# More warming matmuls, a later rotary sum, fuller early filler and spread residual transposes in a two-layer hybrid encoder

## The chip, the cores and the metric

The kernel runs on one core of one Trainium2 chip, as one program launched once. A core has five engines with an instruction stream each: TensorE (PE, matrix products and transposes), VectorE (DVE), ScalarE (ACT), GpSimd (POOL) and SyncE (SP, which here only issues DMAs). Streams run side by side and meet at semaphores. Data lie in on-chip memory, products accumulate in the eight banks of PSUM, and weights come from the chip's main memory by DMA. The metric is the device time of one execution in microseconds (us); the median of the runs counts. The profile is one execution; PE's granted clock is part of it (1.00 is full, 0.50 half).

## The reference

Input: x of 512 tokens by 1024 features in float32, with the parameters of two layers. The tokens form a grid of 8 rows by 64 columns. Cut to what matters:

```
h = x
# layer 0
hn = rmsnorm(h, norm_mix[0])
qa, ka, va, cq, ckv, kr = split(hn @ w_in)                 # 1024 x 1440
qa = axial_rope(rmsnorm(qa per head)); ka = the same       # 8 heads, 2 kv heads of 64
oa = softmax(qa ka^T / 8) va                               # all 512 tokens
qb = rmsnorm(cq) @ w_uq;  kvb = rmsnorm(ckv) @ w_ukv       # 8 heads, 64 + 32 rotary
ob = softmax([q_nope, rope(q_rope)] [k_nope, rope(kr)]^T / sqrt(96)) vb
h = h + concat(oa, ob) @ w_out
h = h + relu(rmsnorm(h) @ w_up)^2 @ w_down                 # width 4096
# layer 1
q, k, v = split(rmsnorm(h, norm_mix[1]) @ w_qkv)           # 16 heads of 64
per query: a window of 8 rows x 16 columns of keys (clamped), softmax(q k^T / 8 + bias) v
h = h + o @ w_out
h = h + relu(rmsnorm(h) @ w_up)^2 @ w_down
return rmsnorm(h, final_norm)
```

The rotary scheme multiplies a vector by a cosine and its partner (the other half of a group of 32) by a sine, and adds the two.

## The kernel before

**Products.** A float32 product is made from two-part operands: each operand is split into a high part (rounded to fp32r) and the rest, and three matmuls stand for one product: high by high, high by low, low by high (`mm3`, L422 to L425 for the projections, L1366 to L1368 for the last down product, L311 to L313 in the other MLP parts). A matmul of 128x128 against 512 columns is the usual piece. Weights come in chunks: SP issues the DMA into `raw` (L180), ACT copies the high part `whi` (L189), DVE or POOL subtracts to get the low part `wlo` (L190, L200). There are four raw buffers and three of each part (`chunk`, L173).

**Order.** The order on each engine isn't that of the text. A scheduler takes the program's operations and lays out each engine's stream by its own model of when each is ready, so that an edit may or may not move an instruction. PSUM's banks are shared out by role: three `mm` banks for products, two `s` banks for scores, two `t` banks for transposes, one `o` bank for outputs and odds and ends. `Fill` keeps generators of products and lays them between attention steps, as many as a credit in us allows; a product of three matmuls counts 0.69.

**Beginning.** `idle_work` (L133) issues matmuls of ones by ones before any data is there. The gains `norm_mix` are turned by one transpose (L142) and copied to `gT` (L143). `make_x(k)` (L457 to L467) turns a block of x by four transposes (L461), and ACT (L465) and DVE (L466) split it, times the gain; DVE keeps the raw turn as `hT` (L467). `load_w(k)` (L619) brings one 128x768 chunk of `w_in`. Then `first_product` (L990) runs the first projection with six banks, eight steps along the depth each; `norm()` (L1012) is called inside of it, which sums squares over partitions by products with a column of ones (L443) and so gets the row factors. Layer 1's first projection goes through `norm()` as well.

**Layer 0, heads A.** `heads_A` (L903) runs eight heads in four units of two. At the first head of a unit it starts the next unit's rotary: `rope_q(t + 1)` (L524). `rope` (L473 to L486) issues eight DMAs on SP that bring the partners (L479), the product with the cosine, the product with the sine (L484, on POOL when `far`), and the sum on DVE (L485). The result is split by ACT and DVE (L537) and three SP DMAs put the parts where the two heads of the unit want them. `attend` (L832) makes a head in four score steps: scores (L876), the row's maximum in a DVE instruction that also copies them (L880), exponential on ACT, reciprocal (L883), scale on POOL (L884), then the turn of the weights by PE (L843), its split by ACT (L845) and DVE (L846), and the products with the values (L856 to L866). After each step it calls `done(i)`.

**Layer 1, heads C.** `projC(t)` makes q, k and v of two heads; k of each head is split (L1167, L1168) and copied to the other half of the partitions by a DMA on POOL's queue (L1170); v is turned by transposes (L1176). `attend_C` (L1187) runs 16 heads. Per head: scores of two blocks (L1201), the second half of the previous head's turns (`second`), filler (`step(n, 0)`), the previous head's value products (`finish`, L1235), scores of the other two blocks, filler, the first turns (L1220) and their split (L1224, L1225), filler. In front of every second head it makes sure that the filler of that pair's projection is done. `step` (L1295) sets the credit of a filler: 2.85 us, 5.6 from head 14 on, where the output projection is the filler.

**Last MLP.** `last_mlp` (L1316) makes the down product with the weights as the stationary operand: per step k along the depth four matmul triples j = 0..3. In the first group of steps, four transposes at a time (L1380) turn a block of the residual `hT` back into rows, into a `t` or an `mm` bank in turn, and ACT copies each block out (L1381). There are four blocks for each of two halves c.

Of the kernel before, what the change touches and what calls it, by code (L numbers as in the profile page):

```python
# [16 lines left out]
S = 512  # L17
# [18 lines left out]
def encoder_kernel(ctx: ExitStack, tc: tile.TileContext, ins, out, dbg=None):  # L36
# [51 lines left out]
    def ob():  # L88
        return bank("o", 1)
# [42 lines left out]

    def idle_work(n):  # L133
        b = ob()
        for _ in range(n):
            PE.matmul(b[:, 0:P], ones, ones, start=True, stop=True)

    idle_work(6)
    act0 = tiny(1)
    ACT.activation(act0, zeros, AF.Copy)  # L140
    gp = stb()
    PE.transpose(gp[:, 0:16], gs.t[0:16, 0:P], ident[0:16, 0:16])  # L142
    DVE.tensor_copy(gT[:, 0:16], gp[:, 0:16])  # L143

# [27 lines left out]

    def chunk(parts, nk, ncol, heads=None, eng=None):  # L173

# [13 lines left out]
        if heads is None:  # L188
            ACT.activation(hi[:, 0:m], raw[:, 0:m], AF.Copy)  # L189
            (eng or DVE).tensor_tensor(lo_[:, 0:m], raw[:, 0:m], f32(hi[:, 0:m]), op=ALU.subtract)  # L190
# [282 lines left out]
    def rope(src, cos, sin, mask, n=P, far=False):  # L473
# [9 lines left out]
        POOL.tensor_tensor(c[0:n, :], src[0:n, :], cos[0:n, :], op=ALU.mult)  # L483
        (POOL if far else DVE).tensor_tensor(sh[0:n, :], sh[0:n, :], sin[0:n, :], op=ALU.mult)  # L484
        DVE.tensor_tensor(c[0:n, :], c[0:n, :], sh[0:n, :], op=ALU.add)  # L485
        return c  # L486
# [37 lines left out]
    def rope_q(t):  # L524

        QA.append(Slot())
        rt = rope(QS[t // 2].t[:, S * (t % 2) : S * (t % 2) + S], cosA, sinA, sw16, far=t > 0)
        q = QA[t].pair()
        if t == 0:
            for e in range(2):  # L530
                a, z = 64 * e, 64 * (1 - e)
                ACT.activation(q[a : a + 64, e, :], rt[a : a + 64, :], AF.Copy)
                DVE.tensor_tensor(q[z : z + 64, e, :], rt[a : a + 64, :], f32(q[a : a + 64, e, :]), op=ALU.subtract)
        else:
            lo = scratch(F32R)
            ACT.activation(q[:, 0, :], rt, AF.Copy)
            DVE.tensor_tensor(lo, rt, f32(q[:, 0, :]), op=ALU.subtract)  # L537
            SP.dma_start(f32(q[0:64, 1, :]), f32(q[64:128, 0, :]))
            SP.dma_start(f32(q[64:128, 1, :]), f32(lo[64:128, :]))
            SP.dma_start(f32(q[64:128, 0, :]), f32(lo[0:64, :]))  # L540

# [77 lines left out]
    def load_w(k):  # L619
        W[k] = chunk([(0, 768, rows(w_in, k, 1)[:, :, 0:768])], 1, 768)  # L620

# [8 lines left out]
    load_x(1)  # L630
    make_x(0)
    make_x(1)
    load_w(2)
# [269 lines left out]
    def heads_A():  # L903
        for h in range(8):
            t, e, kv = h // 2, h % 2, h // 4
            if e == 0 and t < 3:
                rope_q(t + 1)
                if t == 2:
                    for s_ in QS + [rpA]:
                        s_.free()  # L910
            q, k = QA[t].pair(), KA[kv].pair()

            def done(i, t=t, e=e):
                if i == 3 and e:
                    QA[t].free()
                    if t % 2:
                        KA[t // 2].free()
# [72 lines left out]
    def first_product(l):  # L990
# [38 lines left out]
        def plain():  # L1029
            four = product(w, 0, xp, tiles(0, 512), ev, lambda n: [mmb(), mmb(), mmb(), sbk()])  # L1030
            two = product(w, 0, xp, tiles(512, 256), ev, lambda n: [sbk(), ob()], kstep=4)
            for n, _ in enumerate(four):
                if n == 11:
                    norm()
                if n == 14:
                    x7.sums(0, fill_x)
                    x7.sums(1, fill_x)
# [257 lines left out]
    def step(n, z):  # L1295
        if n == 14 and z == 0:
            for s_ in X:
# [3 lines left out]
            for cols in ([0, 1, 2], [3, 4, 5], [6, 7]):  # L1301
                out_proj(w_out1, 0, ok, cols, "out")
        fill.run(2.85 if n < 14 else 5.6)

# [11 lines left out]
    def last_mlp(l):  # L1316
# [37 lines left out]
        def down(k0, c, up, tail):  # L1354
# [5 lines left out]
            def run():  # L1360
# [9 lines left out]
                for k in range(nk - tail):  # L1370
                    for j in range(4):
                        use(k, j)
                        if k0 == 0:
                            later(c, 4 * k + j)
                        if k0 == 0 and k < 2 and j % 2:

                            i = 2 * k + j // 2
                            b = stb() if flip[0] == 0 else mmb()
# [89 lines left out]
```

## Time and profile before

| what | us |
|---|---|
| median of 3 runs | 1223.73 |
| the runs | 1222.79, 1223.73, 1228.44 |
| the profiled execution, whole time | 1228.26 |
| its span, first to last instruction | 1226.5 |
| mean granted clock of PE in it | 0.992 |
| PE busy | 1193.7 (97%) |
| DVE busy | 814.6 (66%) |
| ACT busy | 628.3 (51%) |
| POOL busy | 420.2 (34%) |

In the lines of the profile, each group is: engine, operation, output <- input by the names of the program, shape, and how often; L12 is line 12 of the kernel. In the timeline, the first number is the start in us from the start of the span, the second the length (of the whole run, where xN stands behind it), and a bracket holds how long the engine had stood idle just before and what ended it. In a list of waits, the three numbers are us in total, times, and the longest. A table of windows has, for each stretch, its length, then busy us and instructions of each engine, PE's clock as granted, the DMA share and GB/s. Matmuls overlap in the records: the pace is read from start to start.

The stages in this execution, by time: the first products up to about 45 us, layer 0's attention and output projection up to about 267, its MLP up to about 575, layer 1's first projection up to 637, its attention up to 851, and the output projection, the last MLP and the final norm up to 1226.5.

### The profile page before, as it was taken

How to read it: one execution, taken by the hardware profiler on the slowest of the kernel's cores; microseconds unless marked ns; L12 is line 12 of the kernel's file. 1: busy time of each engine (PE TensorE's matmuls, PEld its weight loads, DVE VectorE, ACT ScalarE, POOL GpSimd, SP SyncE). 2: the span in 40 equal slices, each digit the busy share in tenths (PEclk: the TensorE clock that was granted, in tenths of full speed). 3: DMA queues.
4: the chain of work that ended last, by engine and by line, in shares of the span. 5: the costliest groups of instructions: out<-in, count | busy, mean ns of one | idle time of the engine just before them, and what ended most of it. 6: DMA issues, size and time to landing. Idle time of an engine off the chain costs nothing.

```text
span 1226.5 us, 18425 instructions
## 1 busy us (share of the span) xinstructions
PE 1193.7 (97%) x6626; PEld 1004.5 (82%) x6626; DVE 814.6 (66%) x1433; ACT 628.3 (51%) x1051; POOL 420.2 (34%) x535
## 2 busy tenths in 40 slices
PE   9998999999999999999999999999989999999997
PEld 7676788887899889898877788777768988988985
DVE  4587888878677347457576677766974762763764
ACT  4477676664355226336345565554463641461543
POOL 3256242205374155254002222220333912723700
PEclk9999999999999999999999999999999999999999
DMA  6223314212235224247233334323222342241432
GB/s 235 71 57 102 74 48 129 69 52 69 77 88 154 86 61 139 85 139 241 85 88 106 108 108 117 108 95 103 70 68 60 96 155 61 80 157 48 121 121 69
DMA packets 107259, 122.69 MB, mean 100 GB/s; under 512 B 8115, under 2 KB 81120, under 8 KB 107168
## 3 DMA queue, kind: packets, MB, share of 16 engines
q1 hardware_dynamic: 104880, 116.15, 31.5%
q0 software_dynamic: 1536, 4.21, 1.4%
q10 hardware_dynamic: 752, 1.15, 0.3%
q8 instruction: 52, 0.85, 0.3%
q14 instruction: 39, 0.32, 0.1%
HBM read 104.32 MB, written 6.29 MB: 90 GB/s over the span
## 4 chain that ended last, share of the span: by engine, by line
PE 77%; DVE 8%; ACT 4%; POOL 3%; issue 3%; DMA 2%; SPq 1%; ACTq 0%; DVEq 0%; POOLq 0%
PE mm L425 8%; PE mm L423 8%; PE mm L424 8%; PE o L856 2%; PE s L876 2%; PE s L425 2%; PE s L424 2%; PE s L423 2%; PE t L843 2%; PE mm L1367 2%; PE mm L1368 2%; PE mm L1366 2%; PE mm L313 1%; PE mm L311 1%; PE mm L312 1%
## 5 line engine op out<-in xcount | busy, mean ns | idle before, releaser
L190 DVE TENSOR_TENSOR wlo<-raw,whi 128x1024 fp32r<-128x1024 f32 (+2 forms) x141 | 157.9, 1122 | 159.8 <-ACT whi L189 158.3
L189 ACT ACTIVATE whi<-raw 128x1024 fp32r<-128x1024 f32 (+2 forms) x145 | 137.2, 948 | 175.9 <-PE o L424 38.4
L423 PE MATMUL mm<-a,whi 128*128 128x512 f32 x524 | 213.3, 409 | 0.8 <-ACT whi L189 0.4
L424 PE MATMUL mm<-a,whi 128*128 128x512 f32 x524 | 209.2, 399 | 0.0
L425 PE MATMUL mm<-a,wlo 128*128 128x512 f32 x524 | 208.5, 400 | 0.1
L237 DVE TENSOR_TENSOR wlo<-raw,whi 128x896 fp32r<-128x896 f32 x104 | 130.7, 1257 | 106.2 <-ACT whi L236 105.8
L236 ACT ACTIVATE whi<-raw 128x896 fp32r<-128x896 f32 x104 | 98.8, 950 | 160.1 <-POOL raw L233 27.9
L231 POOL TENSOR_TENSOR raw<-raw 128x128 f32<-128x128 f32 x104 | 61.7, 593 | 267.5 <-DMA raw<-in_ffn_w_up_dram 221.1
L425 PEld LDWEIGHTS mm<-a,wlo 128*128 128x128 f32 x524 | 99.4, 190 | 23.7 <-issue 1.7
L423 PEld LDWEIGHTS mm<-a,whi 128*128 128x128 f32 x524 | 99.4, 190 | 21.9 <-issue 0.9
L424 PEld LDWEIGHTS mm<-a,whi 128*128 128x128 f32 x524 | 99.9, 191 | 19.8 <-issue 1.7
L233 POOL TENSOR_TENSOR raw<-raw 128x128 f32<-128x128 f32 x104 | 96.4, 927 | 8.1
L232 POOL TENSOR_TENSOR raw<-raw 128x256 f32<-128x256 f32 x104 | 90.5, 870 | 8.2
L1209 POOL TENSOR_SCALAR p<-p,ti 128x256 f32<-128x256 f32 x64 | 35.3, 555 | 137.8 <-DVE ti L1208 120.7
L313 PE MATMUL mm<-a,wlo 128*128 128x256 f32 x280 | 79.2, 283 | 2.1 <-DVE wlo L237 2.1
L311 PE MATMUL mm<-a,whi 128*128 128x256 f32 x280 | 78.5, 280 | 0.0
L312 PE MATMUL mm<-a,whi 128*128 128x256 f32 x280 | 78.5, 280 | 0.0
L884 POOL TENSOR_SCALAR p<-p,ti 128x512 f32<-128x512 f32 x64 | 46.9, 735 | 87.9 <-DVE ti L883 76.8
L313 PEld LDWEIGHTS mm<-a,wlo 128*128 128x128 f32 x280 | 52.7, 188 | 3.6 <-DVE wlo L237 3.6
L312 PE MATMUL t<-a,whi 128*128 128x256 f32 x192 | 53.9, 281 | 0.0
L311 PE MATMUL t<-a,whi 128*128 128x256 f32 x192 | 53.8, 280 | 0.0
L313 PE MATMUL t<-a,wlo 128*128 128x256 f32 x192 | 53.7, 280 | 0.0
(306 smaller groups left out, 3040.9 us busy)
## 6 DMA issues: line engine op xcount, KB each, us to landing
raw<-in_ffn_w_down_dram SPq DMA_DIRECT2D x64, 512.0 KB
raw<-in_ffn_w_up_dram SPq DMA_DIRECT2D x104, 256.0 KB
raw<-in_od_w_qkv_dram SPq DMA_DIRECT2D x64, 192.0 KB
raw<-in_ffn_w_up_dram SPq DMA_DIRECT2D x12, 512.0 KB
raw<-in_ev_w_in_dram SPq DMA_DIRECT2D x12, 384.0 KB
bias<-bx SPq DMA_DIRECT2D x16, 256.0 KB
a<-a POOLq DMA_DIRECT2D x16, 256.0 KB, 3.5
a<-a SPq DMA_DIRECT2D x10, 256.0 KB
```

What stands on the lines that cost most here:

```text
L189: ACT.activation(hi[:, 0:m], raw[:, 0:m], AF.Copy)
L190: (eng or DVE).tensor_tensor(lo_[:, 0:m], raw[:, 0:m], f32(hi[:, 0:m]), op=ALU.subtract)
L232: POOL.tensor_tensor(r[:, 4:6], r[:, 2:3].to_broadcast([P, 2, P]), r[:, 0:7:6], op=ALU.add)
L233: POOL.tensor_tensor(r[:, 7], r[:, 3], r[:, 5], op=ALU.subtract)
L236: ACT.activation(hi[:, 0:896], raw[:, 128:1024], AF.Copy)
L237: DVE.tensor_tensor(lo[:, 0:896], raw[:, 128:1024], f32(hi[:, 0:896]), op=ALU.subtract)
L311: PE.matmul(o, wh, x[:, 0], start=kp == 0 and z == 0, stop=False, skip_group_check=True)
L312: PE.matmul(o, wh, x[:, 1], start=False, stop=False, skip_group_check=True)
L313: PE.matmul(o, wl, x[:, 0], start=False, stop=kp == self.np - 1, skip_group_check=True)
L423: PE.matmul(o, wh, xh, start=first, stop=False)
L424: PE.matmul(o, wh, xl, start=False, stop=False)
L425: PE.matmul(o, wl, xh, start=False, stop=last)
```

## The change

1. At the start, `idle_work` issues 11 instead of 6 calls, and four more calls stand between the turns of the first two blocks of x. The copy of the turned gains goes from DVE to ACT; the high part of the very first weight chunk is copied by DVE instead of ACT.
2. In layer 0's heads A, the rotary of units 1 to 3 returns its two products; the sum, its split and the three DMAs are issued by `sum_q` from `done(2)` of the unit's first head, that is three score steps later in the text. The slots of the unrotated q come free there too.
3. Layer 1's first projection calls `norm()` at step 13 instead of 11.
4. In layer 1's attention the filler's credit is 3.4 for the first two heads, 2.85 up to head 12, and 4.0 from head 13 on; the output projection joins the filler at head 13 instead of 14.
5. In the last MLP the residual's transposes stand once in each of the first four steps, behind the fourth triple, instead of twice in each of the first two.

```diff
--- before.py
+++ after.py
@@ -130,17 +130,17 @@
     POOL.dma_start(gs.t[48:56, 0:P], ins["final_norm"].rearrange("(k p) -> k p", p=P))
 
 
-    def idle_work(n):
-        b = ob()
+    def idle_work(n, b=None):
+        b = b or ob()
         for _ in range(n):
             PE.matmul(b[:, 0:P], ones, ones, start=True, stop=True)
 
-    idle_work(6)
+    idle_work(11)
     act0 = tiny(1)
     ACT.activation(act0, zeros, AF.Copy)
     gp = stb()
     PE.transpose(gp[:, 0:16], gs.t[0:16, 0:P], ident[0:16, 0:16])
-    DVE.tensor_copy(gT[:, 0:16], gp[:, 0:16])
+    ACT.activation(gT[:, 0:16], gp[:, 0:16], AF.Copy)
 
     def gmix(l, k):
         return gT[:, 8 * l + k : 8 * l + k + 1]
@@ -170,7 +170,7 @@
         return y
 
 
-    def chunk(parts, nk, ncol, heads=None, eng=None):
+    def chunk(parts, nk, ncol, heads=None, eng=None, first=False):
 
         raw = wp.tile([P, 1024], F32, tag="raw", bufs=4, name=nm("raw"))
         r3 = raw[:, 0 : nk * ncol].rearrange("p (k n) -> p k n", k=nk)
@@ -186,7 +186,10 @@
         m = nk * ncol
         v = lambda t: t[:, 0:m].rearrange("p (k n) -> p k n", k=nk)
         if heads is None:
-            ACT.activation(hi[:, 0:m], raw[:, 0:m], AF.Copy)
+            if first:
+                DVE.tensor_copy(hi[:, 0:m], raw[:, 0:m])
+            else:
+                ACT.activation(hi[:, 0:m], raw[:, 0:m], AF.Copy)
             (eng or DVE).tensor_tensor(lo_[:, 0:m], raw[:, 0:m], f32(hi[:, 0:m]), op=ALU.subtract)
         else:
 
@@ -482,6 +485,8 @@
         c = scratch()
         POOL.tensor_tensor(c[0:n, :], src[0:n, :], cos[0:n, :], op=ALU.mult)
         (POOL if far else DVE).tensor_tensor(sh[0:n, :], sh[0:n, :], sin[0:n, :], op=ALU.mult)
+        if far:
+            return c, sh
         DVE.tensor_tensor(c[0:n, :], c[0:n, :], sh[0:n, :], op=ALU.add)
         return c
 
@@ -523,21 +528,32 @@
 
     def rope_q(t):
 
+
         QA.append(Slot())
-        rt = rope(QS[t // 2].t[:, S * (t % 2) : S * (t % 2) + S], cosA, sinA, sw16, far=t > 0)
+        src = QS[t // 2].t[:, S * (t % 2) : S * (t % 2) + S]
+        if t:
+            hold["rope"] = rope(src, cosA, sinA, sw16, far=True)
+            return
+        rt = rope(src, cosA, sinA, sw16)
         q = QA[t].pair()
-        if t == 0:
-            for e in range(2):
-                a, z = 64 * e, 64 * (1 - e)
-                ACT.activation(q[a : a + 64, e, :], rt[a : a + 64, :], AF.Copy)
-                DVE.tensor_tensor(q[z : z + 64, e, :], rt[a : a + 64, :], f32(q[a : a + 64, e, :]), op=ALU.subtract)
-        else:
-            lo = scratch(F32R)
-            ACT.activation(q[:, 0, :], rt, AF.Copy)
-            DVE.tensor_tensor(lo, rt, f32(q[:, 0, :]), op=ALU.subtract)
-            SP.dma_start(f32(q[0:64, 1, :]), f32(q[64:128, 0, :]))
-            SP.dma_start(f32(q[64:128, 1, :]), f32(lo[64:128, :]))
-            SP.dma_start(f32(q[64:128, 0, :]), f32(lo[0:64, :]))
+        for e in range(2):
+            a, z = 64 * e, 64 * (1 - e)
+            ACT.activation(q[a : a + 64, e, :], rt[a : a + 64, :], AF.Copy)
+            DVE.tensor_tensor(q[z : z + 64, e, :], rt[a : a + 64, :], f32(q[a : a + 64, e, :]), op=ALU.subtract)
+
+    def sum_q(t):
+        q = QA[t].pair()
+        rt, sh = hold["rope"]
+        DVE.tensor_tensor(rt, rt, sh, op=ALU.add)
+        lo = scratch(F32R)
+        ACT.activation(q[:, 0, :], rt, AF.Copy)
+        DVE.tensor_tensor(lo, rt, f32(q[:, 0, :]), op=ALU.subtract)
+        SP.dma_start(f32(q[0:64, 1, :]), f32(q[64:128, 0, :]))
+        SP.dma_start(f32(q[64:128, 1, :]), f32(lo[64:128, :]))
+        SP.dma_start(f32(q[64:128, 0, :]), f32(lo[0:64, :]))
+        if t == 3:
+            for s_ in QS + [rpA]:
+                s_.free()
 
     r0 = keep([P, 4], F32, "r0")
     r0sq = keep([P, 4], F32, "r0sq")
@@ -617,7 +633,7 @@
     W = {}
 
     def load_w(k):
-        W[k] = chunk([(0, 768, rows(w_in, k, 1)[:, :, 0:768])], 1, 768)
+        W[k] = chunk([(0, 768, rows(w_in, k, 1)[:, :, 0:768])], 1, 768, first=k == 0)
 
     def use_w(k, m):
         hi, lo = (z[:, 0, mt0[m] : mt0[m] + P] for z in W[k])
@@ -629,6 +645,7 @@
     load_w(1)
     load_x(1)
     make_x(0)
+    idle_work(4, banks[5])
     make_x(1)
     load_w(2)
     load_x(2)
@@ -905,12 +922,11 @@
             t, e, kv = h // 2, h % 2, h // 4
             if e == 0 and t < 3:
                 rope_q(t + 1)
-                if t == 2:
-                    for s_ in QS + [rpA]:
-                        s_.free()
             q, k = QA[t].pair(), KA[kv].pair()
 
             def done(i, t=t, e=e):
+                if e == 0 and t < 3 and i == 2:
+                    sum_q(t + 1)
                 if i == 3 and e:
                     QA[t].free()
                     if t % 2:
@@ -1030,7 +1046,7 @@
             four = product(w, 0, xp, tiles(0, 512), ev, lambda n: [mmb(), mmb(), mmb(), sbk()])
             two = product(w, 0, xp, tiles(512, 256), ev, lambda n: [sbk(), ob()], kstep=4)
             for n, _ in enumerate(four):
-                if n == 11:
+                if n == (11 if l == 0 else 13):
                     norm()
                 if n == 14:
                     x7.sums(0, fill_x)
@@ -1293,14 +1309,14 @@
     w_out1 = ins["od_w_out"][0]
 
     def step(n, z):
-        if n == 14 and z == 0:
+        if n == 13 and z == 0:
             for s_ in X:
                 s_.free()
             ok = [s_.pair() for s_ in O]
             assert len(ok) == 6
             for cols in ([0, 1, 2], [3, 4, 5], [6, 7]):
                 out_proj(w_out1, 0, ok, cols, "out")
-        fill.run(2.85 if n < 14 else 5.6)
+        fill.run(3.4 if n < 2 else 2.85 if n < 13 else 4.0)
 
     attend_C(step)
     fill.until("out")
@@ -1372,9 +1388,9 @@
                         use(k, j)
                         if k0 == 0:
                             later(c, 4 * k + j)
-                        if k0 == 0 and k < 2 and j % 2:
-
-                            i = 2 * k + j // 2
+                        if k0 == 0 and j == 3:
+
+                            i = k
                             b = stb() if flip[0] == 0 else mmb()
                             for q in range(4):
                                 PE.transpose(b[:, q * P : (q + 1) * P], hT[:, 4 * c + q, i * P : (i + 1) * P], ident)
```

## The prediction

> **What bounds the kernel now.** I read the first rows of the page first: which engine is busy, and which owns the chain that ended last.
>
> ```profile
> span 1226.5 us, 18425 instructions
> PE 1193.7 (97%) x6626; PEld 1004.5 (82%) x6626; DVE 814.6 (66%) x1433; ACT 628.3 (51%) x1051; POOL 420.2 (34%) x535
> PE 77%; DVE 8%; ACT 4%; POOL 3%; issue 3%; DMA 2%; SPq 1%; ACTq 0%; DVEq 0%; POOLq 0%
> ```
>
> TensorE is the bound from end to end. The change takes no product away, so it can gain only where PE stands still or runs slowly. The waits of PE come next (total us, times, longest):
>
> ```profile
> PE t L1380 <- ACT a L1381: 4.1, 1, 4.1
> PE o L856 <- DVE a L846: 2.7, 2, 2.5
> PE s L1201 <- DMA a<-a: 2.7, 2, 1.9
> PE t L142 <- DMA a<-in_norm_mix_dram: 1.5, 1, 1.5
> PE t L443 <- DVE acc L438: 0.9, 1, 0.9
> ```
>
> Each part of the change aims at one of these rows. The third view is the table of windows, because the granted clock is not 1.00 everywhere (columns: PE, weight load, DVE, ACT, POOL busy, then the clock):
>
> ```profile
> 112.27:115.68 3.41, 1.12 (x5) 0.48 (x3) 1.38 (x5) 1.79 (x6) 2.51 (x3) 1.00 0.21 77
> 115.68:119.09 3.41, 3.10 (x14) 2.90 (x15) 2.68 (x6) 2.21 (x5) 2.44 (x3) 0.50 0.53 108
> 904.16:907.57 3.41, 0.32 (x3) 0.32 (x4) 3.41 (x6) 3.41 (x7) 0.00 (x0) 1.00 0.01 2
> 907.57:910.98 3.41, 3.41 (x13) 2.72 (x11) 2.15 (x4) 1.45 (x4) 1.23 (x3) 0.50 0.27 77
> ```
>
> A stretch of 3.41 us in which PE mostly waited is followed by one of the same length at half clock, in which PE does 1.7 us less work. There are four during the work: at 115.7 and 907.6 above, at 668.6 behind the wait on L1201, and at 870.0 behind the stretch with L443. A wait of 2 us or more can thus cost itself plus 1.7 us. Last, the timeline of PE at the beginning:
>
> ```profile
> 1.00 2.93 PE L136 MATMUL o<-ones 128*128 128x128 f32 x12 [1.00 <-POOL zeros L109]
> 5.44 0.26 PE L142 MATMUL t<-cst,a 16*128 16x16 f32 x1 [1.52 <-DMA a<-in_norm_mix_dram]
> 5.63 2.19 PE L461 MATMUL t<-cst,a 128*128 128x128 f32 x8
> 9.27 0.63 PE L423 MATMUL mm<-a,whi 128*128 128x512 f32 x1
> 13.88 0.40 PE L425 MATMUL s<-a,wlo 128*128 128x512 f32 x1
> 15.17 0.48 PE L423 MATMUL mm<-a,whi 128*128 128x512 f32 x1
> ```
>
> The first matmuls last 0.63 us and start 0.425 us apart; from 13.3 on they last 0.39 and start 0.233 apart: PE is cold for 13.3 us.
>
> **The base of the sum.** The profiled execution took 1228.26 us: the span of 1226.5 and 1.76 around it. It stands 4.53 above the median 1223.73 of the runs (1222.79 to 1228.44). The runs thus lie two to three half-clock windows apart, and not every execution need have all four.
>
> **Start: more warming matmuls, one copy to ACT, one to DVE.** Twelve records of L136 in 2.93 us, 0.21 us apart, become 22: they end at about 5.70, not 3.93. The transpose L142 waited until 5.44 for its DMA, so that only 0.26 us are new on the path. The second call adds eight records between the transposes of the first and second row block. If the clock opens at about 6.5, these cost 8 x 0.107 (half of 0.21) = 0.85 us, in place of the 0.44 us that PE waited for L189 anyway; the first product comes at about 8.05 instead of 8.25, its 18 matmuls take 18 x 0.233 = 4.2 us, and the second block of products begins, 0.35 us of transposes later, at 12.6 instead of 15.17: a gain of 2.6. If the clock stays half until 13.28, the ten extra records and the eight push the first product to 9.85 and the second block to 15.95: a loss of 0.8. The DVE copy of 128x768 isn't in the trace; DVE's 128x512 copy L467 (0.68) bounds it from below, the 128x768 subtraction L190 (0.95) from above. I take 0.95 (same width): from the landing of the weights at 5.16 it ends by 6.1, before the first x block is ready, as L465 ended at 7.47. gT on ACT (0.17 on DVE) delays L465 by nothing, for the same transposes end later. Later weight chunks (10.76, 13.18, 15.64) land ahead of a PE that runs 2.6 earlier. I take -2.6.
>
> In the trace the stretch from 6.45 to 9.86 (1.4 us of transposes, then products, 88% busy) did not open the clock; the stretch from 9.86 to 13.28, all products, did. The Trainium skill, page "TensorE: Matmul & The Clock Gate", Part 1 (The HAM clock gate), says that the gate watches a free-running window and opens after about one busy window of 3.4 us; the trace's stretches of 3.41 us agree, and by this rule alone the clock is open by 1.0 + 2x3.41 = 7.8. The same page, Part 4 (PE-mode transpose), says that transposes don't count as busy in the same way: by that, the work before 5.70 must fill a window alone, and where it doesn't, the start goes as in rival 1. The first of the two stretches bears the second rule out.
>
> **Rotary sums.** Chain of the third rope: eight DMAs of L479 on SP from 104.30, issued over 5.78 us, land by 111.46; POOL then works off L200 and L605 before L484 at 113.28; DVE stands 2.03 us at the sum, and L846 behind it, which PE awaits, is late.
>
> ```profile
> 113.28 1.26 POOL L484 TENSOR_TENSOR sc<-sc,a 128x512 f32<-128x512 f32 x1
> 114.58 0.69 DVE L485 TENSOR_TENSOR sc<-sc,sc 128x512 f32<-128x512 f32 x1 [2.03 <-POOL sc L484]
> 115.99 1.86 PE L856 MATMUL o<-a,a 128*128 128x256 f32 x7 [2.54 <-DVE a L846]
> ```
>
> The diff issues the sum three score steps later. But the order on the engines isn't that of the text. Set side by side, the two kernels' orders on DVE, POOL, SP and ACT are the same around the third sum: it keeps its place between the scale of a second score tile (L880) and the reciprocal L883. The 2.54 us and the half-clock window stay: 0. Only for the first two ropes does something move: the split L537 of the first by one score step, the sum of the second behind one L880, where DVE stood 0.66 us at 96.57. Their three SP DMAs follow as late; no score matmul of these units waited for them. Bounds 0 and -0.67; I take -0.4, since PE's next waits there are under 0.5. The slots QS and rpA come free later, and nothing that takes them has moved.
>
> **Norm at product step 13.** PE's and DVE's orders at L443 are again the same: 0. The 0.92 us and the window at 870.0 stay.
>
> **Filler in layer 1's attention.** The waits are 1.93 us at 667.37 and 0.77 at 788.61, both for the POOL DMA that copies K. From K's last product to its first score PE had 6.65 us of work at the first of these, now 8.28; K's split also comes forward on DVE, ahead of V's, but it can start no earlier than its product: I put K some 1.1 us late no more (bounds 0.45 and 1.85), so 0.8 is left to gain. The second wait goes (0.77): its distance grows most. With a wait of 1.1 the window before 668.6 is no longer mostly idle, so its 1.7 goes. Together -3.3; bounds -4.4 (first wait gone) and, where the waits for DVE, ACT and POOL of these heads (1.1+0.5+0.4+0.4 in all) double, +2.4. The whole filler is the same work moved; at the end 24 instead of 42 products are left between the last scores and the last transposes, and where one filler of 15 hid the flip before, nine did elsewhere.
>
> **Residual transposes.** In the first four steps of the last layer's down product the transposes stood 6 matmuls apart, now 12.
>
> ```profile
> 897.97 0.39 PE L1366 MATMUL mm<-whi,a 128*128 128x512 f32 x1
> 907.25 0.86 PE L1380 MATMUL t<-cst,hT 128*128 128x128 f32 x4 [4.07 <-ACT a L1381]
> 911.08 0.49 PE L1366 MATMUL mm<-whi,a 128*128 128x512 f32 x1
> ```
>
> The first evacuation L1381 starts at 906.63 behind L189, L1009, L286 and L725 on ACT, and PE wants its buffer from 903.2 on. In the new order ACT has one more L286 (0.52) before it: it ends at about 907.7. PE reaches the third transposes at 897.97 + 36x0.233 + 2x0.35 = 907.06 and waits 0.7. The fifth step then begins at 897.97 + 48x0.233 + 4x0.35 + 0.7 = 911.25; before, at 911.08 + 24x0.233 = 916.67. Gain 5.4 (3.7 of waiting, 1.7 of half clock). The weights for it stood ready at 906.7. Bounds -2 (each of three evacuations costs one wait) and -5.8.
>
> **Sum:** -2.6 - 0.4 + 0 - 3.3 - 5.4 = -11.7, so 1216.6 for an execution like the profiled one, with the windows at 115.7 and 870.0 left. From the median, without any half-clock term: 2.6 + 0.4 + 1.6 + 3.7 = 8.3, so 1215.4; with the one window that a wait of 4.07 us all but always opens, 1213.7. I take 1215.0.
>
> **Rivals.**
> 1. The clock doesn't open early, because neither 4.7 us of L136 nor the transposes fill one of the gate's stretches: the start loses 0.8 instead of gaining 2.6, so 1218.4. For it: 88% busy from 6.45 to 9.86 didn't open it. Against: most positions of the stretch lie over 2.7 us within the warming work.
> 2. The wait of the transposes is replaced: ACT's evacuations, queued behind L189 and L286, hold each of the next three sets, and the residual part gives 2: 1218.5 to 1219.
> 3. Slower: in layer 1's attention V's transposes (L1176) and the flips (L1220) share the two t banks, and with more filler in the first heads they stand closer; if each of 16 heads waits 0.9 us (the longest waits on L1201, L1220 and L1176 now, 0.2 to 0.5 each, together), attention gives +14.4 against -6.7 of the other parts: 1223.7 + 7.7 = 1231.4. The kernel is slower than before from 6.7/16 = 0.42 us a head. Against: both kernels' orders hold the same transposes, and DVE is busy for 66% only.
> 4. The sum and norm parts do take effect on the chip, through times rather than order: -4.2 more, 1211.
>
> **How the numbers follow.** A measurement tells about 0.5% (6.1 us) from nothing: faster is below 1217.6, slower above 1229.8. Forecast 0.50 (1215 +- 2.5), rival 1 0.22, rival 2 0.10, rival 3 0.12, rival 4 0.06. Faster: 0.50 + 0.06 + 0.04 of rivals 1 and 2 at their near ends = 0.60; slower 0.10 of rival 3; the rest, 0.30, is the same. The range takes in the bounds of the parts from the median: below 1223.7 - 2.6 - 0.7 - 2.7 (both K waits) - 4.1 - 4.2 (rival 4) = 1209.4, above 1223.7 + 0.8 + 2.4 - 2 = 1224.9. It leaves out most of rival 3.
>
> **What would show it.** Right: clock full and 0.39-us products before 9.9; second block at 12.6; the 2.5-us wait at L856 still there; the wait at 667 near 1.1; no row L1380 <- L1381 over 1. Wrong: matmuls of 0.63 after 10; a new half-clock stretch between 640 and 851; a wait on L1176 or L1220 that recurs in each head.

## The result and the profile after

The changed kernel takes 1221.44 us (median of 22 runs, 1219.18 to 1223.61), the kernel before 1225.29 beside it (22 runs, 1221.49 to 1228.44). The ratio is 0.9968, 95% interval 0.9959 to 0.9977: 3.9 us (2.8 to 5.0) faster. The forecast was 8.7 us faster. The change is real, but less than half of the forecast, and below the 0.5% that had been set as the bound for no change.

One thing in the description ahead of the prediction is wrong: `first_product` isn't the first projection but the first piece of each MLP's up product, and `norm()` is called in there. So part 3 of the change moves the norm inside of the last layer's MLP, at 868 us. No term of the sum rests on it.

The page of the changed kernel (profiled execution 1220.60 us, one of the faster ones):

```profile
span 1218.8 us, 18461 instructions
PE 1189.6 (98%) x6644; PEld 1003.4 (82%) x6644; DVE 814.0 (67%) x1433; ACT 628.3 (52%) x1051; POOL 411.5 (34%) x535
PE 78%; DVE 9%; ACT 4%; issue 3%; SPq 2%; POOL 2%; DMA 2%; DVEq 0%; POOLq 0%; ACTq 0%
```

TensorE is the bound as before, but its waits (total us, times, longest) are others. The line numbers are those of the changed kernel: L1217 is L1201 of before (scores of layer 1's heads), L1221 is L1205 (DVE's reading of the scores), L1192 is L1176 (V's turn), L873 and L863 are L856 and L846, L883 is L866 (the addition of a head's two value halves), L446 is L443.

```profile
PE s L1217 <- DVE ti L1221: 4.0, 7, 1.1
PE o L873 <- DVE a L863: 2.8, 2, 2.6
PE t L1192 <- DVE sc L1189: 1.7, 3, 1.0
PE o L873 <- DVE sc L883: 1.4, 1, 1.4
PE t L446 <- DVE acc L441: 0.9, 1, 0.9
```

Of these, the kernel before has the first and the third as

```profile
PE s L1201 <- DVE ti L1205: 1.1, 4, 0.5
PE t L1176 <- DVE sc L1173: 0.4, 2, 0.3
```

and the fourth was 0.45. The row of L1380 (4.1) and the row of K's DMA (2.7) are gone. The second and the last are nearly as they were. Windows (PE, weight load, DVE, ACT and POOL busy, then the granted clock):

```profile
111.44:114.85 3.41, 0.82 (x4) 0.47 (x5) 1.52 (x4) 1.76 (x5) 2.51 (x3) 1.00 0.00 0
114.85:118.27 3.42, 3.42 (x16) 2.91 (x16) 2.81 (x6) 2.30 (x5) 2.00 (x3) 0.50 0.62 123
902.60:906.01 3.41, 3.33 (x17) 2.43 (x15) 3.41 (x6) 3.41 (x7) 0.00 (x0) 1.00 0.01 1
906.01:909.42 3.41, 3.37 (x17) 2.79 (x18) 3.12 (x5) 1.91 (x3) 1.61 (x1) 1.00 0.25 77
```

The half-clock stretch behind the third rotary sum stays. Around the residual's transposes PE is now busy all the time, at full clock. At the beginning:

```profile
0.99 4.92 PE L136 MATMUL o<-ones 128*128 128x128 f32 x22 [0.99 <-POOL zeros L109]
6.49 1.06 PE L136 MATMUL o<-ones 128*128 128x128 f32 x8
8.85 0.40 PE L426 MATMUL mm<-a,whi 128*128 128x512 f32 x1
12.71 0.48 PE L426 MATMUL mm<-a,whi 128*128 128x512 f32 x1
```

The clock is full from 5.6 us; the products last 0.40 at 8.85, and the second block of them begins at 12.71, not at 15.17.

### The profile page after: what moved, and what is told of

Same layout as the page of the kernel before. It is cut to its first block, busy times and chain, and to the rows that moved or that the text cites. A ratio compares the mean times of both kernels' runs of the same rounds, so it can differ in the third digit from the quotient of the medians.

```text
span 1218.8 us, 18461 instructions
## 1 busy us (share of the span) xinstructions
PE 1189.6 (98%) x6644; PEld 1003.4 (82%) x6644; DVE 814.0 (67%) x1433; ACT 628.3 (52%) x1051; POOL 411.5 (34%) x535
## 4 chain that ended last, share of the span: by engine, by line
PE 78%; DVE 9%; ACT 4%; issue 3%; SPq 2%; POOL 2%; DMA 2%; DVEq 0%; POOLq 0%; ACTq 0%
PE mm L428 7%; PE mm L426 7%; PE mm L427 7%; PE s L428 2%; PE s L427 2%; PE s L426 2%; PE s L893 2%; PE o L873 2%; PE mm L316 2%; PE mm L314 2%; PE mm L315 2%; PE mm L1384 2%; PE mm L1383 2%; PE mm L1382 2%; PE t L860 2%
## 5 line engine op out<-in xcount | busy, mean ns | idle before, releaser
L240 DVE TENSOR_TENSOR wlo<-raw,whi 128x896 fp32r<-128x896 f32 x104 | 128.1, 1232 | 106.9 <-ACT whi L239 100.7
L234 POOL TENSOR_TENSOR raw<-raw 128x128 f32<-128x128 f32 x104 | 62.4, 600 | 271.5 <-DMA raw<-in_ffn_w_up_dram 204.7
L236 POOL TENSOR_TENSOR raw<-raw 128x128 f32<-128x128 f32 x104 | 90.7, 872 | 8.1
L235 POOL TENSOR_TENSOR raw<-raw 128x256 f32<-128x256 f32 x104 | 87.9, 845 | 8.2
```

What stands on the lines that cost most here:

```text
L235: POOL.tensor_tensor(r[:, 4:6], r[:, 2:3].to_broadcast([P, 2, P]), r[:, 0:7:6], op=ALU.add)
L236: POOL.tensor_tensor(r[:, 7], r[:, 3], r[:, 5], op=ALU.subtract)
L240: DVE.tensor_tensor(lo[:, 0:896], raw[:, 128:1024], f32(hi[:, 0:896]), op=ALU.subtract)
```

## The experiments

Parts are numbered as in the change: 1 start, 2 rotary, 3 norm, 4 filler, 5 residual. Part 3 has no run of its own. The run without it (parts 1 and 5) and the one with it (parts 1, 2, 3 and 5) have the same order of operations and shapes on all five engines from 130 us on, so it moves nothing. All ratios are to the kernel before, run beside each.

### Each part alone

Part 5 alone:

```diff
-                        if k0 == 0 and k < 2 and j % 2:
-                            i = 2 * k + j // 2
+                        if k0 == 0 and j == 3:
+                            i = k
```

> The kernel before with the residual's transposes spread alone (part 5). Theory (the whole change was worth only 3.9 us in the medians because two parts cost time, while this one gives what was forecast): 3.7 us of waiting at L1380 gone, and the half-clock stretch behind it in most executions, so 4.5 to 5.5 us faster, ratio 0.9955 to 0.9963; no wait of L1380 over 1 us. Rival (the gain was given back by other waits on ACT's evacuations or weights in the same product): 2 us or less, ratio 0.998 or above, with a new row on L1366 to L1368.

Measured: 0.9951 (0.9937 to 0.9966), 1220.17 us, so 6.0 us faster; no wait at L1380 is left among the longer ones. A little more than the theory, and its rival is out.

Part 1 alone:

```diff
-    idle_work(6)
+    idle_work(11)
...
-    DVE.tensor_copy(gT[:, 0:16], gp[:, 0:16])
+    ACT.activation(gT[:, 0:16], gp[:, 0:16], AF.Copy)
...
+                DVE.tensor_copy(hi[:, 0:m], raw[:, 0:m])
...
+    idle_work(4, banks[5])
```

> The kernel before with the start of the change alone (part 1). Theory (as in the profile after, where the second block of products began at 12.71 instead of 15.17): 2.0 to 2.6 us faster, ratio 0.9979 to 0.9984, clock full from before 7 us. Rival (the gate's stretch lies differently in every execution, and the profile of the whole change showed a lucky one): between 1 us faster and 0.8 slower on the median, ratio 0.9992 to 1.0007, and a profile with half clock up to 9 or later.

Measured: 0.9970 (0.9959 to 0.9982), 3.7 us faster, more than the theory; clock full from 7.0. In all fifteen profiles of kernels with part 1 the clock was full from between 4.1 and 7.0 us on; in the four without it from 4.5, 9.9, 12.4 and 13.3. So the old start is a matter of luck, and the new one isn't. The Trainium skill, page "TensorE: Matmul & The Clock Gate", Part 1 (The HAM clock gate), says that the gate's window runs free and that one busy window of 3.4 us opens it: these profiles agree with it.

The gain of the start itself is smaller than the time measured. The second block of products begins between 12.2 and 13.3 us in the fifteen profiles (12.8 on average), and at 11.8, 13.4, 14.6 and 15.2 in the four (13.7): about 1 us. The profile that the theory went by, with 15.17, is the latest of the four.

Part 4 alone:

```diff
-        if n == 14 and z == 0:
+        if n == 13 and z == 0:
...
-        fill.run(2.85 if n < 14 else 5.6)
+        fill.run(3.4 if n < 2 else 2.85 if n < 13 else 4.0)
```

> The kernel before with the fuller filler in layer 1's attention alone (part 4). Theory (the K waits of 1.93 and 0.77 us go, but the waits of L1201 for DVE at L1205 grow from 1.1 to 4.0 in sum and those of L1176 for DVE at L1173 from 0.4 to 1.7, since the splits of the next pair's K now stand between two scores of a head): 1 to 3 us slower, ratio 1.0008 to 1.0025, K wait gone. Rival (the forecast: the K wait goes and nothing takes its place): 2 to 3.3 us faster, ratio 0.9973 to 0.9984.

Measured: 1.0009 (1.0000 to 1.0019), 1.1 us slower; the scores' waits for DVE are 3.8 us in sum, those of V's turn 1.6, and the wait for K's DMA is gone. That is the theory's low end, and the forecast for this part is out.

Part 2 alone:

```diff
-        DVE.tensor_tensor(c[0:n, :], c[0:n, :], sh[0:n, :], op=ALU.add)
-        return c
+        if far:
+            return c, sh
...
+                if e == 0 and t < 3 and i == 2:
+                    sum_q(t + 1)
```

> The kernel before with the later rotary sum alone (part 2). Theory (the third sum stays where it was and its 2.5 us wait with it; the second sum is moved among the evacuations so that L856 waits 1.4 us for the pair's addition L866): 0.7 to 1.5 us slower, ratio 1.0006 to 1.0012. Rival (the forecast: a gain of 0.4 at the first two units): ratio 0.9995 to 0.9999. Second rival (the 1.4 us belonged to the earlier start of the change, which shifted POOL's work against PE's, not to the sum): no wait on L866 of over 0.6 here, ratio 0.999 to 1.0002.

Measured: 0.9999 (0.9986 to 1.0011). The new wait on the pair's addition is there (1.5 us, once), so the second rival is out; the time can't tell the theory from the forecast.

### Which part eats the gain

The single parts add up to 8.7 us, the whole change gave 3.9. Parts 1 and 5 together (the two diffs above):

> The kernel before with the start and the residual's transposes alone (parts 1 and 5). The single parts measured -3.7 and -6.0 us, the filler +1.1 and the rotary -0.1, which sums to -8.7, but the whole change gave -3.9. Theory a (the rotary or the filler costs more once the start is earlier): these two add up here, -8.5 to -10.5 us, ratio 0.9914 to 0.9931. Theory b (the two gains don't add, since both are partly saved half-clock stretches): -5 to -6.5 us, ratio 0.9947 to 0.9959.

Measured: 0.9921 (0.9906 to 0.9936), 1214.94 us: 9.7 us faster. The two add up, and the changed kernel is slower than these two parts of it. Without part 4 (parts 1, 2, 3, 5):

> The changed kernel without its filler part (parts 1, 2, 3 and 5). If the filler is what eats the gain (theory a1): -8 to -10 us against before, ratio 0.992 to 0.9935, waits on L1201's line for DVE back at about 1.1 us. If the rotary eats it (a2): -4 to -6, ratio 0.995 to 0.9967, with the wait on the pair's addition in heads A of 1.4 us.

Measured: 0.9938 (0.9925 to 0.9951), 1217.51 us, 7.6 us faster: just short of a1's range, and far from a2's. Without part 2 (parts 1, 3, 4, 5):

> The changed kernel without its rotary part (parts 1, 3, 4 and 5). If the filler eats the gain (a1): -4 to -6 us, ratio 0.995 to 0.9967, waits of the scores of layer 1's heads for DVE at 4 us in sum. If the rotary does (a2): -8 to -10 us, ratio 0.992 to 0.9935, and no wait of over 0.6 us on the pair's addition L866.

Measured: 0.9960 (0.9947 to 0.9973), 1220.28 us, as a1 says. These kernels ran on one chip: on top of parts 1 and 5 the filler costs 0.39%, about 4.8 us (give or take 2.4), the rotary 0.17%, 2.1 us (give or take 2.4; the medians of six runs each stand 2.6 apart). Most of what was lost is the filler's.

### What in the filler costs

Parts 1 and 5 with only the early credit:

```diff
-        fill.run(2.85 if n < 14 else 5.6)
+        fill.run(3.4 if n < 2 else 2.85 if n < 14 else 5.6)
```

> Parts 1 and 5, and of the filler's part only the first half: 3.4 us for the first two heads, then as before (2.85 up to head 13, 5.6 after, output projection from head 14). If what harms is that the whole filler runs 3.3 us ahead, so that the splits of K come between the two score pairs of a head: 1 to 3 us slower than the kernel with parts 1 and 5 alone, with waits on the second score pair for DVE of about 1 us in three or more heads. If what harms is the thinner filler at the end (4.0 from head 13): not slower than that kernel, and 1 to 2.7 us faster where the K waits go.

Measured: 0.9967 (0.9954 to 0.9979), by the ratios 5.6 us over parts 1 and 5 alone and by the medians 4.9, more than the 1 to 3 expected. The early credit makes the cost by itself. Parts 1 and 5 with only the late half:

```diff
-        if n == 14 and z == 0:
+        if n == 13 and z == 0:
...
-        fill.run(2.85 if n < 14 else 5.6)
+        fill.run(2.85 if n < 13 else 4.0)
```

> Parts 1 and 5, and of the filler's part only the second half (2.85 to head 12, output projection from head 13, 4.0 after). Theory (only the early credit harms, since it shifts where the splits of Q and K stand against the scores): within 1.2 us of parts 1 and 5 alone, ratio 0.9912 to 0.9932. Rival (the thinner end harms too): 1.5 us or more slower, ratio 0.9935 or above, with new waits after 800 us.

Measured: 0.9929 (0.9911 to 0.9948), 1216.58 us: within the theory's range, and no cost that can be told from the time, though the waits in its profile sum to 4.0 us against 2.5 in the table below. A smaller early credit:

```diff
-        fill.run(2.85 if n < 14 else 5.6)
+        fill.run(3.05 if n < 2 else 2.85 if n < 14 else 5.6)
```

> Parts 1 and 5, and an early credit of 3.05 instead of 3.4 for the first two heads, the rest as before. In DVE's order the splits of Q and K then stand among a head's second scores for two of the seven pairs, against six of seven with 3.4 and none with 2.85. Theory (the loss goes with the number of such pairs): 1 to 2.5 us slower than parts 1 and 5 alone, ratio 0.993 to 0.9942. Rival (the loss comes from running ahead as such, or from the first pair): as large as with 3.4, about 5 us, ratio 0.9955 to 0.997; or no loss and the K wait gained, ratio below 0.992.

Measured: 0.9967 (0.9954 to 0.9980): as dear as 3.4, as the rival says. The theory that the loss goes with the number of pairs falls. The waits say why. These are PE's waits from 637 to 851 us of each profile, in us (the flips are the turns of the weights, L1220 of before):

| kernel | scores for DVE | scores for K's DMA | V's turn for DVE | flips for POOL | sum |
|---|---|---|---|---|---|
| parts 1, 5 | 1.1 | 0.8 | 0.4 | 0.2 | 2.5 |
| parts 1, 3, 4, 5 | 4.1 | - | 1.5 | 1.0 | 6.6 |
| parts 1, 5, credit 3.4 | 4.5 | - | 1.8 | 1.0 | 7.3 |
| parts 1, 5, credit 3.05 | 3.2 | 3.0 | 0.4 | 0.6 | 7.2 |

Each kernel with early filler waits 4.1 to 4.8 us more than the one without, which is most of the time lost (by the ratios 4.8, 5.6 and 5.6 us). With 3.05 the wait for K isn't gone but larger in sum than in any other profile. Where the scores wait, DVE and PE of the kernel with parts 1, 3, 4 and 5 show this (L1166 and L1172 split Q and K, L1209 reads the scores, L1205 writes them):

```profile
676.95 1.40 DVE L1166 TENSOR_TENSOR a<-sc,a 64x512 fp32r<-64x512 f32 x2
678.38 1.40 DVE L1172 TENSOR_TENSOR a<-sc,a 64x512 fp32r<-64x512 f32 x2
679.82 0.42 DVE L1209 CUSTOM_DVE_ANT_0 p<-s,bias 128x256 f32<-128x256 f32 x1
```

```profile
680.31 0.50 PE L1205 MATMUL s<-a,a 128*128 128x256 f32 x2 [1.10 <-DVE ti L1209]
```

The next pair's splits now stand between the scores of a head and their reading, and PE wants the scores' bank back. With the old credit K's split stands between two heads for all seven pairs, Q's for five; with 3.4 K's stands between a head's scores for six of seven. In the kernel with parts 1 and 5, the last reading of a head is followed by both splits, and the next head's readings come behind them:

```profile
676.58 0.42 DVE L1209 CUSTOM_DVE_ANT_0 p<-s,bias 128x256 f32<-128x256 f32 x1
679.28 1.40 DVE L1166 TENSOR_TENSOR a<-sc,a 64x512 fp32r<-64x512 f32 x2
681.26 1.39 DVE L1172 TENSOR_TENSOR a<-sc,a 64x512 fp32r<-64x512 f32 x2
```

The other traces agree. In layer 1's attention of all nineteen profiles, PE's scores waited twenty times for 0.9 us or more for DVE to read earlier ones. Each of these waits is in a kernel whose filler was changed, and each time K's split is among the six DVE instructions ahead of that reading. Without K's split there, the longest such wait is 0.76 us. K's split doesn't always make a long one: behind it there are waits of 0.2 to 0.8 us too. The next two changes were to take DVE's share away. First, Q's subtraction on POOL, in the kernel with parts 1, 3, 4 and 5:

```diff
-                        DVE.tensor_tensor(q[z : z + 64, e, :], n_[a : a + 64, :], f32(q[a : a + 64, e, :]),
-                                          op=ALU.subtract)
+                        POOL.tensor_tensor(q[z : z + 64, e, :], n_[a : a + 64, :], f32(q[a : a + 64, e, :]),
+                                           op=ALU.subtract)
```

> The changed kernel without its rotary part (which measured 0.9960), and the low part of Q in layer 1's heads subtracted on POOL instead of DVE: 1.4 us of DVE less for each pair, where its splits stand ahead of a head's second scores. Theory (the filler's loss is the scores' bank held by a DVE that is busy with the splits): the waits of the scores for DVE fall from 4.1 to 2.5 or less, 1.5 to 3.5 us faster than without the move, ratio 0.9932 to 0.9948. Rival (the loss comes from POOL's scale of the weights and from the DMA of K): DVE's waits may fall, but those for POOL and the DMA grow by as much, ratio 0.996 or above.

Measured: 0.9999 (0.9984 to 1.0014), 4.8 us slower than without the move, and the scores' waits for DVE rose to 6.1. The theory's number is missed the other way, and its premise fails too: DVE's time for the splits fell only from 19.3 to 16.5 us over the stage, not by half. From this kernel, DVE, POOL and PE:

```profile
735.65 2.69 DVE L1172 TENSOR_TENSOR a<-sc,a 64x512 fp32r<-64x512 f32 x2 [0.36 <-ACT a L1171]
```

```profile
734.25 2.66 POOL L1166 TENSOR_TENSOR a<-sc,a 64x512 fp32r<-64x512 f32 x2
```

```profile
739.73 0.54 PE L1205 MATMUL s<-a,a 128*128 128x256 f32 x2 [2.35 <-DVE ti L1209]
```

K's two subtractions on DVE took 2.69 us beside POOL's instead of 1.40. Then Q's low part left out:

```diff
-                        DVE.tensor_tensor(q[z : z + 64, e, :], n_[a : a + 64, :], f32(q[a : a + 64, e, :]),
-                                          op=ALU.subtract)
+                        ACT.activation(q[z : z + 64, e, :], n_[a : a + 64, :], AF.Copy, scale=0.0)
```

> The changed kernel without its rotary part (0.9960), and the low part of Q in layer 1's heads left out: ACT writes zeros in its place, so that DVE has two instructions of 0.69 us less per pair and POOL does not work beside it. Theory (the filler's loss is DVE's splits ahead of a head's scores): the waits of the scores for DVE fall from 4.1 to under 3, 1.5 to 3 us faster than 0.9960, ratio 0.9935 to 0.9948, and clearly more than the same omission gives without the filler. Rival (DVE's share doesn't matter): as large a gain or loss as in the run without the filler, 0.995 to 0.997.

> The control: parts 1 and 5 (0.9921), the filler as before the change, and the same omission of Q's low part. Theory (there the splits stand between two pairs' scores): within 1 us of parts 1 and 5 alone, ratio 0.9913 to 0.993. Rival (DVE's work in the heads costs wherever it stands): 1.5 to 3 us faster, ratio 0.9896 to 0.991.

Measured: 0.9963 (0.9948 to 0.9977) with the filler, no change against 0.9960; 0.9953 (0.9938 to 0.9968) without, 4 us slower than parts 1 and 5 alone. Both theories miss; the first ratio lies where its rival has it, but the same omission did cost time without the filler. The omission is no clean one: ACT's zeros stand in the same chain, and in both kernels PE's own order in the heads has changed with it. With the filler (L1171 splits K, L1208 reads the scores):

```profile
729.90 1.41 DVE L1171 TENSOR_TENSOR a<-sc,a 64x512 fp32r<-64x512 f32 x2 [1.80 <-ACT a L1170]
731.33 0.42 DVE L1208 CUSTOM_DVE_ANT_0 p<-s,bias 128x256 f32<-128x256 f32 x1
```

DVE now stands idle for 1.80 us, since ACT writes K's high part behind the zeros, and only then splits K and reads the scores:

```profile
731.82 0.50 PE L1204 MATMUL s<-a,a 128*128 128x256 f32 x2 [1.40 <-DVE ti L1208]
```

So the likely reading is that it isn't how busy DVE is that counts, but that the reading of the scores stands behind K's split in DVE's stream; whatever makes that split late (DVE's own work, POOL beside it, ACT ahead of it) makes PE wait. That fits all of these runs, but no run took the order alone away, since the scheduler sets it; it is read from the traces, not shown by an edit of its own. Why the control lost 4 us isn't settled: its listed waits in that stage are only 1.4 us more, and its profile, its slowest execution, lies 3.6 us behind that of parts 1 and 5 already at 618 us, ahead of the heads.

### What the forecast looked for, by other means

Parts 1 and 5, and the third unit's sum issued so late that it does move on DVE:

```diff
+                if t == 2 and e == 1 and i == 0:
+                    sum_q(3)
```

> Parts 1 and 5 (which measured 0.9921 of the kernel before), and the third unit's rotary sum issued so late (first score step of the unit's second head) that it does change its place on DVE: behind the split of the turned weights that TensorE awaits, not ahead of it. The first two sums stay as before. Theory (the 2.5 us wait at 114 is that split queued behind the sum, and opens the half-clock stretch that follows): wait and stretch go, 4.2 us less, ratio 0.987 to 0.990. Rival (the wait only moves to the next split, or the last unit's q comes late for its scores): 0 to 1.5 us less, ratio 0.991 to 0.9925.

Measured: 0.9921 (0.9900 to 0.9943), no gain that can be told, and the ratio is the rival's; the runs lie in two groups, three at 1213.6 to 1214.0 and three at 1216.7 to 1218.9. In its profile the wait is 0.5, and there is no half-clock stretch behind it or later in PE's work. But the waiting went to other places: PE's listed waits from 100 to 140 us sum to 2.6, against 2.9 with parts 1 and 5. By the count of PE's instructions this profile stands 2.2 us ahead of that one at 200 us, and 0.7 at 692. So the split does queue behind the sum, and without the long wait the stretch goes; the rival is right that the waiting moves, and the time shows no gain. Then the partners of the third rotary by one shuffle:

```diff
-        if far:
+        if far and not dve:
...
-        rt = rope(QS[t // 2].t[:, S * (t % 2) : S * (t % 2) + S], cosA, sinA, sw16, far=t > 0)
+        rt = rope(QS[t // 2].t[:, S * (t % 2) : S * (t % 2) + S], cosA, sinA, sw16, far=t > 0, dve=t == 3)
```

> Parts 1 and 5, and the partners of the third rotary brought by one shuffle on DVE instead of eight DMAs of SP; products and sum as before. Theory (the sum is late because the DMAs land at 111.5 and POOL's product waits for them): no wait of 2 us at the values of heads A, 3 to 4.2 us less than with parts 1 and 5 alone, ratio 0.9885 to 0.990. Rival (POOL's queue, not the DMAs, is what makes the product late): the wait stays over 1.5 us, ratio 0.991 to 0.993.

Measured: 0.9905 (0.9885 to 0.9925), 1214.06 us. The wait of 2.5 is gone (the longest is 1.1, in four pieces of 2.6 in all) and so is the half-clock stretch at 114; the gain of 2.0 us is between the theory and its rival and not clear of the noise. K's last products ahead of Q's:

```diff
-                for a in range(len(cols) if last else n):
+                for a in (order or range(len(cols))) if last else range(n):
...
-        return product(w_qkv, 0, XP, [(D * z + P * t, P) for z in range(3)], ev, three, stride=D)
+        return product(w_qkv, 0, XP, [(D * z + P * t, P) for z in range(3)], ev, three, stride=D, order=(1, 0, 2))
```

> Parts 1 and 5 (0.9921), with the filler as before the change, and K's last products ahead of Q's in each pair's projection, so that its copy by DMA can start 0.5 to 1.4 us sooner. Theory (the wait for K can be had without running the filler ahead): waits of the scores for the DMA fall from 0.8 to 2.0 to under 0.5, 0.5 to 2 us faster than parts 1 and 5 alone, ratio 0.9905 to 0.9917. Rival (in two of seven pairs K's split now stands between a head's scores, which costs what the K wait gives): ratio 0.992 to 0.9945.

Measured: 0.9929 (0.9911 to 0.9948). No row of waiting for K's DMA is left, the scores' waits for DVE are 1.6, and the time, in the rival's range, can't be told from parts 1 and 5: its profile holds a half-clock stretch of two windows (6.8 us) at 116, where that of parts 1 and 5 holds one. Both together:

> Parts 1 and 5, the third rotary's partners by one shuffle on DVE (with which they measured 0.9905), and K's products ahead of Q's. Theory: both gains add, ratio 0.9885 to 0.990. Rival (K first costs): 0.991 to 0.993.

Measured: 0.9887 (0.9869 to 0.9904), 1211.12 us (1210.87 to 1212.51), in the theory's range: 13.9 us faster than the kernel before and, by the ratios, 10 us faster than the changed one. Its profile shows no half-clock stretch from 5.6 us to the end of PE's work.

## Why the prediction was right or wrong

**Start, -2.6: the mechanism right, the number partly luck.** Measured -3.7 (-2.2 to -5.0). The second block began at 12.71 (forecast 12.6). Rival 1, no early clock, came in none of fifteen profiles. But "at 12.6 instead of 15.17" set the new start against the one execution whose clock opened last; over the profiles the start gives about 1 us. Part of the rest shows in layer 1's attention: without part 1 (and without part 4) the K waits sum to 2.0 to 2.7 us, in three profiles, with part 1 and layer 1's heads as before to 0.8 to 1.2, in five. Why an earlier start shortens them stays open.

**Residual, -5.4: right.** Measured -6.0 (-4.2 to -7.7). In the changed kernel the third transposes, due by PE's pace at 905.53 + 0.23 = 905.76, began 0.3 us late, not 0.7, when ACT's first copy-out had ended at 905.42 + 0.58 = 906.00:

```profile
905.42 0.58 ACT L1397 ACTIVATE a<-t 128x512 f32<-128x512 f32 x1
```

```profile
906.05 0.66 PE L1396 MATMUL t<-cst,hT 128*128 128x128 f32 x4
```

Rival 2 is out.

**Norm, 0: right, but for the stretch.** Same order, same wait of 0.9. The window at 870.0 did not stay in the profile after; 10 of all 19 profiles have it, with part 3 and without. Nor had PE "mostly waited" in the stretch ahead of it: it was busy for 2.41 of 3.41 us.

**Rotary: right for the third sum, wrong for the second.** The third stays, as its row shows (2.58 us, and the half-clock window). But "Bounds 0 and -0.67; I take -0.4" reckoned only with DVE's idle 0.66 us at the second sum and with nothing on the other side. POOL's product and that sum came 1 us later against PE's work (94.91 in a kernel that is 2.7 us ahead there, 96.57 before), and the pair's addition further back on DVE, on which L856 waits for its bank, made 1.4 us of a wait that had been 0.45 (L873 and L883 are L856 and L866):

```profile
98.97 2.14 PE L873 MATMUL o<-a,a 128*128 128x256 f32 x16 [1.44 <-DVE sc L883]
```

In time it is 0 to 2 us slower, by the runs with and without it. Rival 4, in which these two parts gain 4.2 us more, is out.

**Filler, -3.3: this is the step that failed.** Two things in it. First, its terms (0.8 of the first wait, 0.77 of the second, and the window's 1.7) took the profiled execution for the usual one. Five profiles without part 4 (parts 1, 2 and 5 alone, parts 1 and 5, and all but part 4) have K waits of 0.8 to 2.0 us in sum, not 2.7, and none has the half-clock stretch at 668: it was that execution's alone. Second, the bound of +2.4, "where the waits for DVE, ACT and POOL of these heads" double, named the right place, but I took the K wait for what decides, and the waits tripled (2.4 to 7.2). The K wait did go; in its place the scores wait for DVE (1.1 to 4.0) and V's turn waits for DVE (0.4 to 1.7). That is rival 3's place, at 4 to 5 us over 16 heads, about 0.3 a head, below its 0.42, so that the kernel came out faster in spite of it. Its mechanism was only partly that of the rival: the scores' bank, which it did not name, holds most of the wait. I had noted that K's split comes forward on DVE and counted it as a gain for K; what it was put in front of (the reading of a head's scores) I had not asked.

**The sum.** Parts 1 and 5 alone measured 1214.94 us. That the forecast of 1215.0 lies there is chance: its terms are -8.0 for them and -3.7 for the rest, where the runs give -9.7 and about +6. Why the filler costs 1.1 us alone and some 4.8 beside parts 1 and 5 is answered in part only. The waits it adds are much the same, but the K wait it removes is 2.0 to 2.7 us without part 1 and 0.8 to 1.2 with it, so that 1 to 2 us less is won back. The rest of the gap, and why the rotary costs nothing alone, stay open: the intervals (1.2 and 2.4) don't close it, and half-clock stretches that come and go are a guess.

## What to carry to other kernels

When filler between attention steps is moved, ask not only what becomes early enough, but which of the producer's in-order instructions now stand ahead of the instruction that gives a bank back. A wait in one profile is worth its usual size over several executions, a half-clock stretch behind it counts only if it comes each time, and a gain at the start is to be set against the usual start, not the one profiled. If a wait has a cause of its own (here the order of three products, and eight DMAs in place of one shuffle), take that away instead of moving other work until it is covered.

## What the runs showed of the hardware

DVE subtractions of two operands slow down beside POOL's: K's split on 64x512 took 1.10 us on average with Q's split on POOL, 0.69 without (fifteen and fourteen instructions). With Q's split on POOL, six of K's subtractions began 0.4 to 1.3 us before one of POOL's ended; each ended about 0.55 us behind POOL's, however early it had begun, and took 0.95 to 1.80 us. The Trainium skill, page "SBUF — State Buffer", SBUF: two separate sides, says that the port pair that DVE and GpSimd share is locked for a whole instruction and the other one waits; these ends agree with it.

What a wait costs in clock differs from profile to profile (each one execution of another kernel): behind the 2.5 us wait at 114 stands no half-clock stretch in one, a stretch of 3.4 us in eight and one of 6.8 us in seven of the sixteen profiles that have this wait.

A stretch of 3.41 us need not be full to open the clock. With part 5 alone PE was busy for 2.89 us from 1.04 to 4.45, with L136 only, and the clock was full from 4.45 on. With part 2 alone it was busy for 2.95 us from 6.51 to 9.92, 0.8 of it transposes, and that opened the clock too. In the kernel before, 2.97 us from 6.45 to 9.86 with 1.4 us of transposes did not.
